# FFN 1's input projection with seven half-size products for eight (19 of 22 tiles), and another passage to the output projection in both FFNs

## The chip, the core and the metric

One NeuronCore of a Trainium2 chip runs the whole kernel. The metric is the device time of one execution in microseconds. The core has a matrix engine (PE, with its own weight loads PEld), a vector engine (DVE), a scalar engine (ACT), GpSimd (POOL) and SyncE (SP); the last two start most of the DMA transfers here. The engines work through lists of instructions of their own and wait for each other by semaphores.

## The reference

One layer of a decoder trunk over 1056 tokens (1024 of a prompt, 32 of eight sample sequences of 4), in fp32, with D = 1024 and a feed-forward width of 2816. `mod` is a normalisation followed by scale and shift; these and the gates come from a small product of a conditioning vector with a large weight matrix (called ada below, nine sets of 1024 numbers).

```
x += 1/2 * gate1 * swiglu(mod(norm(x), shift, scale), ffn1_w_in, ffn1_w_out)
x += gate2 * W_out(sig(gA) * DiffAttn(h) + sig(gB) * Retention(h))
x += 1/2 * gate3 * swiglu(mod(norm(x), shift, scale), ffn2_w_in, ffn2_w_out)
y  = norm(x)

def swiglu(h, w_in, w_out):          # w_in 1024 x 5632, w_out 2816 x 1024
    a, b = split(h @ w_in, 2, axis=-1)
    return (silu(a) * b) @ w_out
```

## The kernel before

**Products.** An fp32 matrix is kept as a high and a low part (`hh`/`hl` for activations, `..h`/`..l` for weights; `split`: the high part on ACT at L175, the low part on DVE at L185), and each product of two tiles is three matmuls (`mm3`, L234 to L236: high by high, high weight by low activation, low weight by high activation). Activations lie with features on the 128 partitions and the 1056 token columns behind them. The columns are taken in three blocks of 352 (`rb`; the last holds 320 prompt and 32 sample columns), in halves of 528 (HR) or in quarters of 264 (QR).

**Two ways of the input projection.** The 2816 hidden features are 22 tiles of 128. The plain way does a tile with two units (`pa`, `pb`) for each of three blocks, 24 matmuls of 352 columns each: 144 for a tile. `ffn_seven` treats the tile's a- and b-parts, the two halves of the 1024 input features and the two halves of the columns as a 2 by 2 block product and does it with seven products instead of eight: each is 24 matmuls of 264 columns, 168 for a tile. It needs sums and differences of the activation blocks (`sums`, `last_sum`, kept in `gx`, 50.7 KB a partition), of the weight blocks (`weights`, on DVE) and of the results (`p1`, `u2`, `p5` on DVE and ACT).

**FFN 1** (64 to 905 us) is one function, `ffn`: for each of six groups of tiles (`CHUNKS`) the plain input projection, with silu(a) times b split into `gh`/`gl` in on-chip memory, and then that group's part of the output projection (`po`), added to X at once by `residual` (L465 to L472). X stays on the chip. Into both kinds of work `step(more)` places the ada steps that are still open: each loads 512 KB of ada weights, splits them and gives PE four matmuls (`adap`); its three buffers are single.

**FFN 2** (2395 to 3149 us) has two tiles the plain way (`ffn_plain`), 20 by `ffn_seven`, with silu(a) times b written to DRAM (`gd`), and then the output projection of all 22 tiles (`ffn_out`), which reads `gd` back in groups (`gr`, `stage`). X lies in DRAM (`xd`) meanwhile and is read back as Z by eight transfers that POOL issues (L1614) before `ffn_out`.

**What sets the order.** The program is written as loops and generators; a list scheduler of the framework then fixes one order of instructions for each engine, and each engine keeps to it. SP's and POOL's transfers each stand in such an order too, so one that waits for its buffer holds up those behind it. Between the FFNs (905 to 2393 us) lie attention, retention and the mixer, which the change doesn't touch.

## Time and profile before

| | before |
|---|---|
| median of 3 runs | 3152.3 us (3148.41 to 3164.13) |
| the profiled execution | 3151.32 us, span in the trace 3149.6 us |
| matmuls on PE | 19615 |
| PE busy | 3013.9 us, 96% of the span |
| DVE / ACT / POOL busy | 57% / 39% / 16% |

The profile is of one execution. The span is the time from the first to the last instruction in it, so 1.7 us of the execution's own time lie outside. Busy times are those of an engine; an engine that is idle costs nothing unless the end waits for it. A few matmul records are missing from the trace.

### The profile page before, as it was taken

The page shows a single profiled execution, that of the slowest core. Times are in us where ns is not written, and L with a number is a line of the kernel's source. Part 1 is how long each engine was busy: PE and PEld are TensorE (multiplying, and loading weights), DVE is VectorE, ACT ScalarE, POOL GpSimd, SP SyncE. Part 2 cuts the span into 40 slices and gives each one's busy share as a digit, 9 for nine tenths or more (in the row PEclk, how much of TensorE's full clock was granted, in tenths as well). Part 3 has the DMA queues.
Part 4 walks back from the last instruction along what each step waited for, and adds up shares of the span by engine and source line. Part 5 has one row for each costly group of instructions (what it writes and reads, how often), then busy time and mean ns, then how long its engine had stood idle before and what let it go on. Part 6 is the DMA issues. An engine that isn't in the chain of part 4 may idle for free.

```text
span 3149.6 us, 49441 instructions
## 1 busy us (share of the span) xinstructions
PE 3013.9 (96%) x19615; PEld 2872.9 (91%) x19615; DVE 1801.1 (57%) x3555; ACT 1240.6 (39%) x2376; POOL 517.8 (16%) x680
## 2 busy tenths in 40 slices
PE   7999999999999999998999999998899999999998
PEld 3999999999989999998889998887798999999998
DVE  5443434344265666667767766666558755554555
ACT  5422222322244243335556556454445433332112
POOL 2100000000033223213223332232023000000002
PEclk9999999999999999999999999999999999999998
DMA  6232222221122313214121221225651222225321
GB/s 219 61 114 82 87 81 84 88 91 54 59 97 69 103 61 104 82 52 135 56 68 59 74 81 57 74 70 159 202 166 44 78 82 75 78 79 192 103 68 56
DMA packets 270130, 286.73 MB, mean 91 GB/s; under 512 B 14224, under 2 KB 224705, under 8 KB 269898
## 3 DMA queue, kind: packets, MB, share of 16 engines
q1 hardware_dynamic: 248394, 212.28, 22.2%
q0 software_dynamic: 21504, 71.29, 6.4%
q8 instruction: 154, 2.52, 0.3%
q14 instruction: 78, 0.64, 0.1%
HBM read 223.78 MB, written 59.74 MB: 90 GB/s over the span
## 4 chain that ended last, share of the span: by engine, by line
PE 36%; DVE 5%; issue 4%; ACT 4%; DMA 3%; POOL 2%; DVEq 0%; ACTq 0%; POOLq 0%; SPq 0%
PE po L235 3%; PE po L236 3%; PE po L234 3%; PE x L235 2%; PE x L234 2%; PE x L236 2%; PE gp L234 1%; PE gp L236 1%; PE gp L235 1%; PE q L235 1%; PE q L234 1%; PE q L236 1%; DMA k_prompt<-ko 1%; PE s L1319 1%; PE s L1320 1%
## 5 line engine op out<-in xcount | busy, mean ns | idle before, releaser
L494 DVE TENSOR_TENSOR silu<-silu,pb 128x352 f32<-128x352 f32 x66 | 34.4, 521 | 232.1 <-PE pb L236 230.0
L428 POOL TENSOR_TENSOR acc<-acc,sq 128x352 f32<-128x352 f32 x27 | 32.5, 1202 | 799.0 <-ACT sq L427 789.4
L465 DVE SCALAR_TENSOR_TENSOR X<-po,mod,X 128x352 f32<-128x352 f32 (+1 forms) x144 | 81.8, 570 | 111.3 <-PE po L236 110.8
L465 DVE SCALAR_TENSOR_TENSOR Z<-po,mod,Z 128x352 f32<-128x352 f32 (+1 forms) x144 | 81.7, 570 | 96.0 <-PE po L236 95.8
L1325 ACT ACTIVATE P<-s,mx 128x256 f32<-128x256 f32 (+7 forms) x128 | 94.7, 740 | 94.7 <-DVE mx L1323 86.3
L1323 DVE TENSOR_REDUCE mx<-s 128x1 f32<-128x256 f32 (+7 forms) x128 | 96.3, 754 | 2.5
L185 DVE TENSOR_TENSOR c<-s,c 128x512 fp32r<-128x512 f32 x80 | 55.2, 690 | 74.0 <-ACT c L175 73.6
L234 PE MATMUL x<-hh,c 128*128 128x264 f32 x320 | 91.8, 287 | 2.4 <-ACT hh L175 1.7
L175 ACT ACTIVATE gh<-silu 128x352 fp32r<-128x352 f32 x66 | 32.7, 496 | 154.8 <-DVE silu L494 154.6
L236 PE MATMUL x<-hh,c 128*128 128x264 f32 x320 | 91.3, 286 | 1.4 <-DVE c L185 1.4
L235 PE MATMUL x<-hl,c 128*128 128x264 f32 x320 | 91.8, 287 | 0.2 <-DVE hl L185 0.2
L235 PE MATMUL x<-gl,c 128*128 128x264 f32 x320 | 91.2, 285 | 0.0
L234 PE MATMUL x<-gh,c 128*128 128x264 f32 x320 | 91.1, 285 | 0.0
L236 PE MATMUL x<-gh,c 128*128 128x264 f32 x320 | 90.9, 285 | 0.0
L1319 PE MATMUL s<-kk,st 128*128 128x512 f32 (+2 forms) x192 | 69.8, 364 | 16.9 <-ACT P L1325 16.8
L175 ACT ACTIVATE ah<-at 128x512 fp32r<-128x512 f32 (+1 forms) x80 | 44.2, 553 | 57.9 <-PE at L1349 57.4
L493 ACT ACTIVATE silu<-pa 128x352 f32<-128x352 f32 x66 | 30.2, 457 | 92.8 <-PE pa L236 92.8
L234 PE MATMUL gp<-hh,g_1h 128*128 128x352 f32 x192 | 66.0, 344 | 0.0
L234 PE MATMUL gp<-hh,g_0h 128*128 128x352 f32 x192 | 65.4, 340 | 0.0
L1320 PE MATMUL s<-kl,st 128*128 128x512 f32 (+2 forms) x192 | 64.7, 349 | 0.4 <-ACT kl L1285 0.3
L236 PE MATMUL gp<-hh,g_1l 128*128 128x352 f32 x192 | 64.0, 333 | 0.0
L235 PE MATMUL gp<-hl,g_1h 128*128 128x352 f32 x192 | 63.7, 332 | 0.0
(1778 smaller groups left out, 11842.7 us busy)
## 6 DMA issues: line engine op xcount, KB each, us to landing
gr<-gd SPq DMA_DIRECT2D x22, 528.0 KB
ada_0r<-ada_w SPq DMA_DIRECT2D x18, 512.0 KB
ada_1r<-ada_w SPq DMA_DIRECT2D x18, 512.0 KB
ada_2r<-ada_w SPq DMA_DIRECT2D x18, 512.0 KB
ada_3r<-ada_w SPq DMA_DIRECT2D x18, 512.0 KB
st<-state_ret SPq DMA_DIRECT2D x32, 256.0 KB
state_ret_sample<-st POOLq DMA_DIRECT2D x32, 256.0 KB, 2.3
kp<-cache_k SPq DMA_DIRECT2D x64, 128.0 KB
```

The lines of the kernel that those rows point to most:

```text
L175: S.activation(out, in_, AF.Copy, scale=scale)
L185: (eng or V).tensor_tensor(out=l, in0=src, in1=f(h), op=ALU.subtract)
L234: T.matmul(out, wh, xh, start=first and j == 0, stop=False, **kw)
L235: T.matmul(out, wh, xl, start=False, stop=False, **kw)
L236: behind[0] = T.matmul(out, wl_, xh, start=False, stop=last and j == n - 1, **kw).ins
L428: (V if k % 2 else G).tensor_tensor(out=acc[k % 2], in0=acc[k % 2], in1=sq[:], op=ALU.add)
L465: V.scalar_tensor_tensor(out=x[k][:, c0:c0 + n], in0=p_[:, :n], scalar=gt[:, k, 0:1], in1=x[k][:, c0:c0 + n], op0=ALU.mult, op1=ALU.add)
L494: V.tensor_tensor(out=s_[:], in0=s_[:], in1=pb[:, :RB], op=ALU.mult)
L1319: T.matmul(ss[:, a:e], s_[:, qc], k_[:, a:e], start=True, stop=False)
L1320: T.matmul(ss[:, a:e], s_[:, qc], l_[:, a:e], start=False, stop=True)
L1323: V.tensor_reduce(out=mx[:], in_=ss[:, :wd], op=ALU.max, axis=AX.X, negate=True)
L1325: S.activation(pt[:, :wd], ss[:, :wd], AF.Exp, bias=mx[:], accum_out=rs[:, c:c + 1])
```

## The change

FFN 1 gets the structure of FFN 2. Its first three tiles are done the plain way (`ffn_plain`, the first two interleaved), tiles 3 to 21 by `ffn_seven` with two ada steps in each tile (`per` = 2, behind products 0 and 1), and `ffn_out` follows. X goes to DRAM as soon as it stands (`keep1`, three transfers on POOL's queue), gives its memory to `gx`, and is read back by eight transfers on SP's queue.

In both FFNs `ffn_out` has a new first group, of two tiles. Its activations are staged in halves of 528 columns in `hh`/`hl` 4 to 7, which the last tile of `ffn_seven` has read by the end of its second product, through the weights' raw buffers (`wr`); its output projection runs in four quarters of 264 columns (192 matmuls) where three blocks of 352 would take 144. X is read back from SP's queue behind the first output weights (in FFN 2 from POOL's queue before). The accumulation bank of the ada steps has a pool of its own and outlives the others (`stay`).

```diff
-CHUNKS = [[0, 1, 2, 3], [4, 5, 6, 7], [8, 9, 10, 11], [12, 13, 14, 15], [16, 17], [18, 19, 20, 21]]
-CHUNKS2 = [[0, 1, 2, 3], [4, 5, 6, 7], [8, 9, 10, 11], [12, 13, 14, 15], [16, 17, 18, 19], [20, 21]]
+CHUNKS = [[0, 1], [2, 3, 4, 5], [6, 7, 8, 9], [10, 11, 12, 13], [14, 15, 16, 17], [18, 19, 20, 21]]
+CHUNKS2 = [[0, 1], [2, 3, 4, 5], [6, 7, 8, 9], [10, 11, 12, 13], [14, 15, 16, 17], [18, 19], [20, 21]]
...
     def residual(tp, x, k, rb, p_, gt):
+        residual_at(tp, x, k, rb * RB, RB, p_, gt)
+
+    def residual_at(tp, x, k, c0, wd, p_, gt):
+        n = min(wd, SEQ - c0)
...
-    def ffn_out(w, tp, x, wout, gt, after, chunks, homes, bridge=iter(()), more=iter(())):
+    def ffn_out(w, tp, x, wout, gt, after, chunks, reload, bridge=iter(()), more=iter(())):
+        def parts(t, ci, q):
+            return t[(4 if ci % 2 == 0 else 0) + q]
         def stage(ci):
             for q, ft in enumerate(chunks[ci]):
-                r = tp.tile([P, ROWS], F32, tag="gr", name=f"gr{ft}", bufs=2)
-                ld(out=r[:], in_=gd[ft][:, :])
-                split(*(t[:] for t in homes[ci][q]), r[:])
+                if ci == 0:
+                    for c in range(2):
+                        r = w.p.tile([P, 8, P], F32, tag="wr", name=f"gr{ft}{c}", bufs=w.raw)[:].rearrange("p k c -> p (k c)")[:, :HR]
+                        ld(out=r, in_=gd[ft][:, c * HR:(c + 1) * HR])
+                        split(*half(4 + 2 * q + c, 0), r)
+                else:
+                    r = tp.tile([P, ROWS], F32, tag="gr", name=f"gr{ft}", bufs=2)
+                    ld(out=r[:], in_=gd[ft][:, :])
+                    split(parts(hh, ci, q)[:], parts(hl, ci, q)[:], r[:])
                 yield
...
+                if ci == 0:
+                    c, s = divmod(rb, 2)
+                    mm3(p_[:, :QR], ws, [tuple(t[4 + 2 * q + c][:, s * QR:(s + 1) * QR] for t in (hh, hl)) for q in range(nf)])
+                    residual_at(tp, x, o, rb * QR, QR, p_, gt())
...
                 for ct in range(nf):
                     step(more)
                     wt = w.get(rows[:, ct * cw:(ct + 1) * cw], nf, cw, f"wo{ci}_{ct}")
+                    if ci == 0 and ct == 0:
+                        reload()
...
+        def keep1(X, rb, eng):
+            eng(out=xd[:, rbs(rb)].rearrange("(k p) c -> p k c", p=P), in_=X[:, :, rbs(rb)])
+        def entry():
+            yield from norm(tn, X, 2, mods, 1, 0, tp)
+            for rb in range(NRB):
+                keep1(X, rb, st)
+            xs1.close()
+            gx.extend(quarters(tas, side="right"))
+            gx.append(pool(tas, "ta", side="right"))
...
-        ffn(sc, w, tp, x, i["ffn1_w_in"][0], i["ffn1_w_out"][0], lambda: mods[2], after1, CHUNKS, LEAD, to_ret(), more,
-            pre={(0, 0): norm(tp, X, 1, mods, 1, 0), (PQ, 1): norm(tp, X, 2, mods, 1, 0)})
+        ffn_plain(w, tp, win1, [0, 1, 2], LEAD, {(0, 0): norm(tn, X, 1, mods, 1, 0, tp), (PQ, 1): entry()}, todo, more, LEAD)
+        for _ in todo:
+            pass
+        psum(0, 0, 1, True)
+        ffn_seven(w, gx[3], gx, win1, list(range(3, DFF // P)), last_sum(gx[3], gx), more, 2)
+        tas.close()
+        psum(3, 3, 1, True)
+        X1 = pool(sb_, "xb", side="right").tile([P, KT, ROWS], F32, name="X1")
+        x = [X1[:, k, :] for k in range(KT)]
+        def reload():
+            for k in range(KT):
+                ld(out=x[k], in_=xd[k * P:(k + 1) * P, :])
...
+        ffn_out(w, pool(sb_, "t1b", side="right"), x, i["ffn1_w_out"][0], lambda: mods[2], after1, CHUNKS, reload, to_ret(), more)
...
-            for k in range(KT):
-                st(out=x[k], in_=xd[k * P:(k + 1) * P, :])
-            ffn_out(w3, pool(s2, "t3"), x, i["ffn2_w_out"][0], lambda: mods[8], after2, CHUNKS2,
-                    [[(hh[c % 2 * 4 + q], hl[c % 2 * 4 + q]) for q in range(4)] for c in range(len(CHUNKS2))])
+            def reload2():
+                for k in range(KT):
+                    ld(out=x[k], in_=xd[k * P:(k + 1) * P, :])
+            ffn_out(w3, pool(s2, "t3"), x, i["ffn2_w_out"][0], lambda: mods[8], after2, CHUNKS2, reload2)
```

The scheduler's order shows three places. The first is POOL at the start of the program, where the sums of squares of x (`acc`) of the three column blocks are added up; before:

```order
L428 TENSOR_TENSOR acc_0_349<-acc_0_349,sq_2_353 128x352
L786 DMA xn_335<-x_sample 32x1024
L428 TENSOR_TENSOR acc_0_349<-acc_0_349,sq_4_359 128x352
L428 TENSOR_TENSOR acc_0_349<-acc_0_349,sq_6_365 128x352
L428 TENSOR_TENSOR acc_1_640<-acc_1_640,sq_2_644 128x352
```

and now:

```order
L436 TENSOR_TENSOR acc_0_358<-acc_0_358,sq_2_362 128x352
L751 DMA xn_344<-x_sample 32x1024
L436 TENSOR_TENSOR acc_0_358<-acc_0_358,sq_4_368 128x352
L769 DMA xd<-X 128x8x352
L436 TENSOR_TENSOR acc_0_358<-acc_0_358,sq_6_374 128x352
L769 DMA xd<-X 128x8x352
L436 TENSOR_TENSOR acc_1_637<-acc_1_637,sq_2_641 128x352
L769 DMA xd<-X 128x8x352
L436 TENSOR_TENSOR acc_1_637<-acc_1_637,sq_4_647 128x352
```

The three stores of X moved ahead of the sums of blocks 1 and 2: they are issued as soon as X stands and not where `entry` is written.

The second place is PE in tile 12 of FFN 1, where an ada step ends one set of numbers and the next step begins; `x`, `q` and `y` are the accumulators of the seven products, `c2` and `c6` weight blocks. Now:

```order
L244 MATMUL y12_1_3774<-hh7_138,c212_3670 128x264
L390 MATMUL adap3_1_3344<-pick_214,ab_212 128x36
L242 MATMUL x12_0_3769<-gh10_914,c612_3705 128x264
L243 MATMUL x12_0_3769<-gl10_915,c612_3705 128x264
L244 MATMUL x12_0_3769<-gh10_914,c612_3705 128x264
L242 MATMUL x12_0_3769<-gh11_916,c612_3705 128x264
L243 MATMUL x12_0_3769<-gl11_917,c612_3705 128x264
L244 MATMUL x12_0_3769<-gh11_916,c612_3705 128x264
L414 MATMUL adap5_0_3858<-ada5_0_0h_3818,cs_148 18x512
L414 MATMUL adap5_0_3858<-ada5_0_0l_3819,cs_148 18x512
L414 MATMUL adap5_0_3858<-ada5_0_0h_3818,cs_148 18x512
```

The ada matmuls, which before stood among the matmuls of `pa`, `pb` and `po` of FFN 1, now stand behind products 0 and 1 of each seven-product tile, 24 matmuls of 264 columns apart (in this tile the second stands six matmuls into product 2).

The third place is DVE in the first group of FFN 2's output projection, where the results `po` are added to X (there called Z); before:

```order
L185 TENSOR_TENSOR wo1_0l_29321<-wo1_0r_29318,wo1_0h_29320 128x1024
L465 SCALAR_TENSOR_TENSOR Z_28890<-po0_4_0_29124,mod8_5472,Z_28890 128x352
L465 SCALAR_TENSOR_TENSOR Z_28890<-po0_4_1_29138,mod8_5472,Z_28890 128x352
L465 SCALAR_TENSOR_TENSOR Z_28890<-po0_4_2_29152,mod8_5472,Z_28890 128x320
L470 TENSOR_TENSOR rs4_29166<-po0_4_2_29152,mod8_5472 128x32
L472 TENSOR_TENSOR Z_28890<-Z_28890,rs4_29166 128x32
```

and now:

```order
L193 TENSOR_TENSOR wo1_1l_30711<-wo1_1r_30708,wo1_1h_30710 128x1024
L475 SCALAR_TENSOR_TENSOR Z_30272<-po0_4_3_30484,mod8_7027,Z_30272 128x232
L480 TENSOR_TENSOR rs4_30492<-po0_4_3_30484,mod8_7027 128x32
L475 SCALAR_TENSOR_TENSOR Z_30272<-po0_5_0_30495,mod8_7027,Z_30272 128x264
L482 TENSOR_TENSOR Z_30272<-Z_30272,rs4_30492 128x32
L475 SCALAR_TENSOR_TENSOR Z_30272<-po0_5_1_30503,mod8_7027,Z_30272 128x264
L475 SCALAR_TENSOR_TENSOR Z_30272<-po0_5_2_30511,mod8_7027,Z_30272 128x264
L193 TENSOR_TENSOR hl2_141<-gr4_30530,hh2_133 128x1056
```

An output tile takes four accumulating instructions and two short ones on DVE where it took three and two, for half as many hidden tiles, and the low parts of the next group's activations (`hl2<-gr4`) lie between them. In the whole of the new first group DVE has, beside 32 of the accumulating and 16 of the short instructions, five low parts of 1056 columns and two of 1024-column weights in FFN 2; in FFN 1 five, and three (two of them ada's).

## Rows read from the trace of the kernel before

**Rows 1.** The page: busy time, TensorE's granted clock, the last chain.

```profile
PE 3013.9 (96%) x19615; PEld 2872.9 (91%) x19615; DVE 1801.1 (57%) x3555; ACT 1240.6 (39%) x2376; POOL 517.8 (16%) x680
...
PEclk9999999999999999999999999999999999999998
...
PE 36%; DVE 5%; issue 4%; ACT 4%; DMA 3%; POOL 2%; DVEq 0%; ACTq 0%; POOLq 0%; SPq 0%
```

**Rows 2.** Windows of FFN 1 and seven: all engines, PEclk, DMA share, GB/s.

```profile
60.00:905.00 845.00, 832.74 (x5065) 795.19 (x5064) 362.84 (x598) 247.69 (x411) 30.49 (x28) 1.00 0.25 77
2474.00:2857.00 383.00, 383.00 (x3138) 383.00 (x3137) 202.58 (x387) 147.16 (x318) 22.55 (x43) 1.00 0.27 85
```

**Rows 3.** Timeline, DVE: last gate of FFN 1's plain tiles 20 and 21.

```profile
821.75 0.52 DVE L494 TENSOR_TENSOR silu<-silu,pb 128x352 f32<-128x352 f32 x1 [1.72 <-PE pb L236]
...
844.64 0.52 DVE L494 TENSOR_TENSOR silu<-silu,pb 128x352 f32<-128x352 f32 x1 [1.72 <-PE pb L236]
```

**Rows 4.** Timeline, POOL: stores of FFN 2's seven-product tiles, twelve tiles apart.

```profile
2610.88 0.54 POOL L672 DMA_DIRECT2D gd<-p  x1 [17.71 <-DVE p L667]
...
2855.56 0.55 POOL L672 DMA_DIRECT2D gd<-p  x1 [4.91 <-DVE p L667]
```

**Rows 5.** Timeline, PE: first and last of six ada waits (idle in brackets).

```profile
138.65 0.41 PE L406 MATMUL adap<-ada_3h,cs 128*18 128x512 f32 x1 [0.77 <-ACT ada_3h L175]
...
191.28 0.40 PE L406 MATMUL adap<-ada_3h,cs 128*18 128x512 f32 x1 [0.42 <-ACT ada_3h L175]
```

**Rows 6.** Timeline, PE and ACT: FFN 2's passage to the output projection.

```profile
2858.12 0.42 PE L234 MATMUL po<-hh,wo_0h 128*128 128x352 f32 x1 [0.84 <-ACT hh L175]
...
2866.68 0.85 PE L234 MATMUL po<-hh,wo_0h 128*128 128x352 f32 x3 [2.59 <-ACT hh L175]
...
2865.54 1.08 ACT L175 ACTIVATE hh<-gr 128x1056 fp32r<-128x1056 f32 x1 [6.03 <-DMA gr<-gd]
```

**Rows 7.** Windows: that passage (PE alone), four us of it (all engines).

```profile
2858.10:2882.00 23.90, 19.98 (x91) 0.79 0.84 316
...
2870.00:2874.00 4.00, 4.00 (x15) 4.00 (x15) 2.19 (x6) 0.00 (x0) 0.00 (x0) 0.50 1.03 407
```

**Rows 8.** Startup: windows, the later store of X (DMA), one ada load and split.

```profile
20.00:40.00 20.00, 17.57 (x73) 7.58 (x74) 11.90 (x17) 13.63 (x27) 6.24 (x7) 0.91 1.03 344
40.00:60.00 20.00, 14.56 (x36) 5.14 (x35) 15.82 (x20) 13.14 (x24) 8.18 (x5) 0.78 0.86 262
60.00:80.00 20.00, 18.31 (x97) 14.05 (x96) 16.60 (x23) 14.45 (x31) 5.03 (x5) 0.96 0.08 30
...
xd<-Y POOLq DMA_DIRECT2D x3, 1408.0 KB, 6.9
...
44.47 0.37 SPq L203 DMA_DIRECT2D ada_3r<-ada_w  x1
...
54.35 1.04 ACT L175 ACTIVATE ada_3h<-ada_3r 128x1024 fp32r<-128x1024 f32 x1
```

**Rows 9.** Window: FFN 2's entry into the seven products, all engines.

```profile
2439.30:2474.00 34.70, 30.21 (x225) 28.64 (x224) 32.05 (x57) 14.58 (x30) 1.57 (x3) 0.96 0.26 74
```

**Rows 10.** Groups of FFN 1: the parts of an ada step.

```profile
L185 DVE TENSOR_TENSOR ada_3l<-ada_3r,ada_3h 128x1024 fp32r<-128x1024 f32 x14 | 17.1, 1225 | 8.6 <-ACT ada_3h L175 8.6
...
L175 ACT ACTIVATE ada_3h<-ada_3r 128x1024 fp32r<-128x1024 f32 x13 | 13.6, 1050 | 22.8 <-DMA ada_3r<-ada_w 22.8
```

**Rows 11.** Groups of FFN 2's output projection on DVE.

```profile
L465 DVE SCALAR_TENSOR_TENSOR Z<-po,mod,Z 128x352 f32<-128x352 f32 x76 | 43.9, 581 | 53.2 <-PE po L236 53.2
L465 DVE SCALAR_TENSOR_TENSOR Z<-po,mod,Z 128x320 f32<-128x320 f32 x37 | 20.3, 550 | 35.4 <-PE po L236 35.4
L185 DVE TENSOR_TENSOR hl<-gr,hh 128x1056 fp32r<-128x1056 f32 x16 | 20.1, 1256 | 12.1 <-ACT hh L175 12.1
L472 DVE TENSOR_TENSOR Z<-Z,rs 128x32 f32<-128x32 f32 x38 | 7.2, 190 | 1.1
L470 DVE TENSOR_TENSOR rs<-po,mod 128x32 f32<-128x32 f32 x38 | 6.8, 180 | 0.0
```

More of the change, by code (lines that the diff above doesn't have):

```diff
@@ L126, in build, with psum @@
     banks = [None]
-    def psum(mm, aux, big):
+    bigs = [None]
+    def psum(mm, aux, big, stay=False):
         if banks[0]:
             banks[0][0].close()
+        if not stay:
+            if bigs[0]:
+                bigs[0][0].close()
+            es = ExitStack()
+            bigs[0] = (es, pool(es, "psb", space=PSUM), big)
         es = ExitStack()
-        banks[0] = (es, pool(es, "ps", space=PSUM), mm, aux, big)
+        banks[0] = (es, pool(es, "ps", space=PSUM), mm, aux)
     psum(3, 3, 1)
@@ L143, in big_ps @@
     def big_ps(name):
-        return banks[0][1].tile([P, 1024], F32, tag="big", name=name, bufs=banks[0][4])
+        return bigs[0][1].tile([P, 1024], F32, tag="big", name=name, bufs=bigs[0][2])
     xd = dr.tile([KT * P, ROWS], F32, name="xd")
@@ L470, in residual @@
             V.tensor_tensor(out=t[:].rearrange("p (b t) -> p b t", t=TS),
[L471 removed]
+                            in0=p_[:, n:wd].rearrange("p (b t) -> p b t", t=TS), in1=bc(gt, k), op=ALU.mult)
             V.tensor_tensor(out=xs, in0=xs, in1=t[:], op=ALU.add)
[L474 to L530 removed]
@@ L532, in ffn_plain @@
-    def ffn_plain(w, tp, win, fts, lead, pre, back=iter(()), more=iter(())):
+    def ffn_plain(w, tp, win, fts, lead, pre, back=iter(()), more=iter(()), quiet=0):
         ws = {}
@@ L542, in ffn_plain @@
             pb = unit(ws[q][1], rb, f"pb{ft}_{rb}")
-            for _ in range(2 - rb % 2):
+            for _ in range((q, rb) == (quiet - 1, 2) if q < quiet else 2 - rb % 2):
                 step(more)
@@ L692, in ffn_out @@
             rows = wout[f0 * P:(f0 + nf) * P, :]
-            g = homes[ci]
             nxt = stage(ci + 1) if ci + 1 < len(chunks) else iter(())
@@ L698, in one @@
                 cc = (o * P) % cw
-                mm3(p_[:, :RB], [(wt[0][:, q, cc:cc + P], wt[1][:, q, cc:cc + P]) for q in range(nf)],
-                    [(g[q][0][:, rbs(rb)], g[q][1][:, rbs(rb)]) for q in range(nf)])
-                residual(tp, x, o, rb, p_, gt())
+                ws = [(wt[0][:, q, cc:cc + P], wt[1][:, q, cc:cc + P]) for q in range(nf)]
+                if ci == 0:
+                    c, s = divmod(rb, 2)
+                    mm3(p_[:, :QR], ws, [tuple(t[4 + 2 * q + c][:, s * QR:(s + 1) * QR] for t in (hh, hl)) for q in range(nf)])
+                    residual_at(tp, x, o, rb * QR, QR, p_, gt())
+                else:
+                    mm3(p_[:, :RB], ws, [tuple(parts(t, ci, q)[:, rbs(rb)] for t in (hh, hl)) for q in range(nf)])
+                    residual(tp, x, o, rb, p_, gt())
             if ci < len(chunks) - 1:
@@ L706, in ffn_out @@
                     wt = w.get(rows[:, ct * cw:(ct + 1) * cw], nf, cw, f"wo{ci}_{ct}")
+                    if ci == 0 and ct == 0:
+                        reload()
                     for o in range(ct * cw // P, (ct + 1) * cw // P):
-                        for rb in range(NRB):
+                        for rb in range(4 if ci == 0 else NRB):
                             one(wt, o, rb)
-                    next(nxt, None)
+                        if o % 2:
+                            next(nxt, None)
                 run(nxt)
@@ L769, in build @@
     bridge = []
-    with ExitStack() as sc:
+    with ExitStack() as sc, ExitStack() as sb_:
         xp = pool(sc, "x1", side="right")
@@ L775, in build @@
         V.tensor_tensor(out=pick[:], in0=quarter(0), in1=quarter(9), op=ALU.add)
-        X = xp.tile([P, KT, ROWS], F32, name="X")
+        xs1, tas, gx = ExitStack(), ExitStack(), []
+        X = pool(xs1, "xa", side="right").tile([P, KT, ROWS], F32, name="X")
+        tn = pool(xs1, "n1", side="right")
         tp = pool(sc, "t1")
-        x = [X[:, k, :] for k in range(KT)]
         with ExitStack() as s2:
@@ L801, in build, with back @@
                         (7, "scale", gff2, False), (6, "shift", None, False), (8, "half", None, False)])
-        def after1(tp, rb):
-            yield from norm(tp, X, rb, mods, 4, 3)
-            (st if rb == 2 else ld)(out=xd[:, rbs(rb)].rearrange("(k p) c -> p k c", p=P), in_=X[:, :, rbs(rb)])
+        def keep1(X, rb, eng):
[7 more added lines that the diff above has]
+            gx.append(pool(tas, "ta", side="right"))
+        def back():
+            while not gx:
+                yield
+            yield from sums(gx[3], gx)
         def rv_pair(r):
```

84 lines of the change are left out of this document (15 added, 69 removed).

## The prediction, on record before the run

> **What bounds the kernel now.** I read the page first: PE is busy 96% of the span, the next engine, DVE, 57%, and PE's granted clock is at its upper level in all slices but the last [rows 1]. The chain that ended last gives PE only 36%, far less than that; it shows one path and is no account of where the span goes. So the question for each stage is how many matmuls it has, what one costs, and where PE stands still. The windows answer the last: FFN 1's 845 us hold 832.7 us of PE work with DVE busy 43%, the seven-product stretch of FFN 2 holds 383.0 of 383.0 with DVE at 53% [rows 2]. Both stages are PE's, so fewer PE cycles there are time, as long as no other engine takes over.
>
> What a tile costs in each way is read from events one tile apart, not from counts of records, since some are missing. The last gate of a plain tile without an ada step is at 821.75, the next one's at 844.64: 22.9 us for 144 matmuls, 159 ns for one of 352 columns [rows 3]. Twelve seven-product tiles lie between the stores at 2610.88 and 2855.56: 244.68 / 12 = 20.4 us for 168 matmuls, 121.4 ns for one of 264 columns [rows 4].
>
> **Tiles 3 to 21 of FFN 1 by seven products.** 22.9 - 20.4 = 2.5 us for a tile, times 19: **-47.5**. The gain in columns is an eighth, in time 11%: the two prices lie on a line of 0.427 ns a column and 8.7 ns a matmul, and that fixed part is paid 168 times for 144. The Trainium skill, page "TensorE: Matmul & The Clock Gate", section "Back-to-back issue gap", speaks against the change: it gives a stream of weight loads and matmuls some 81 ns at 128 columns and 131 ns at 512. Estimated on a line between them that page would give 110 ns at 352 and 99 ns at 264, so 15.9 us for a plain tile and 16.6 for a seven-product one, +13 us in all. The trace does not agree with that page: it has 159 and 121 ns.
>
> **The ada steps.** Their matmuls are the same ones in another place. What goes is six waits in the first group of FFN 1's output projection, where PE stood for a split; the first is 0.77, the last 0.42, all six 3.1 us [rows 5]: **-3.1**. What comes is two steps a tile through single buffers. Step B stands one product (24 x 0.1214 = 2.9 us) behind step A, and its splits can't start before A's matmuls are done: 1.05 on ACT and 1.22 on DVE, 2.3 us [rows 10], so 0.6 us is left for the queue on DVE. From below nothing; from above each of 19 tiles waits as those six did on average, 19 x 0.51 = 9.7. I take **+2**, near the lower end, since 2.3 is under 2.9. If a wait comes, the seven's next product on PE is late, and nothing else.
>
> **The passage to the output projection in FFN 2.** Before, PE waits 0.84 us for the first split part of `hh`, and 2.59 for a later one, whose transfer came 6.03 us after ACT was free for it [rows 6]. The 23.9 us from 2858.1 hold 91 matmuls, at 159 ns 14.5 us of work, and late in them the granted clock is 0.50, the lower of the two levels (1.2 GHz), after an engine that stood still [rows 7]. So 9.4 us and the first wait are lost, 10 us. The cause in the trace is transfers: Z and `gr` together kept the share of the DMA engines at 1.03 [rows 7]. Now two half-size tiles are staged while PE is in the last seven-product tile, and Z is behind the first weights on SP. **-10**, if PE goes from the one to the other without a stop. Z's and `gr`'s bytes are then under way in products 5 and 6 and the new first group (6 + 23 us); before they took some 20 us at about 400 GB/s [rows 7]; I cost them at nothing. If that cover is too short, `po` results wait for X, PE's three accumulators fill up, and up to the same 10 us come back.
>
> **The new first group** is PE work of 192 x 0.1214 = 23.3 us for 144 x 0.159 = 22.9: +0.4 for each FFN, **+0.8**. But DVE gets more to do. From 581 ns at 352 columns and 550 at 320 the slope is 0.97 ns a column, so (an estimate) 496 ns at 264 and 465 at 232. An output tile is 3 x 0.496 + 0.465 + 0.18 + 0.19 = 2.3 us, eight 18.6; five low parts of 1.256 are 6.3 [rows 11], two weights or ada low parts of 1.22 [rows 10] 2.4, and small ones some 0.8: 28.2 against 23.3 of PE in FFN 2; in FFN 1 one low part more, 29.4, against 23.3 and two ada steps (eight matmuls of 512 columns, on the line above 1.8 us), 25.1. So DVE is the longer by 4 to 5 us. Three accumulators let it lag by 3 x 0.73 = 2.2 us, and chunk 1, with twice the matmuls for a result, lets it catch up. I take **+3 for each**. From below nothing (the first results may meet an idle DVE); from above 10 each, the loss of the old passage.
>
> **X stored at startup.** In FFN 1 X now goes out and comes back. The scheduler puts the three stores of 1408 KB among POOL's first sums, in the first 60 us of the kernel. There the DMA engines are full: their share is 1.03 from 20 to 40 us at 344 GB/s, 0.86 to 60, 0.08 after that, while an ada load issued at 44.47 is split only at 54.35 [rows 8]. PE is at 73% from 40 to 60, waiting for these loads. 4.3 MB at 344 GB/s are 12.6 us of transfer. If all of it came before loads that PE waits for, the start would end 12.6 us later; if it fell behind them into the empty time after 60, nothing. The Trainium skill, page "Trainium Kernel Development and Optimization", section "Key Constraints", says that transfers started from SP and from POOL run on the same 16 engines and interleave. By that page the stores are taken from the loads' rate. I take **+2.5**: a part of the loads is done before X stands, so the stores can only be in the way of the rest. What is late next is ada's first two sets of numbers, and with them FFN 1's first matmul.
>
> **Entry into the seven products.** The sums of activations need DVE while the plain tiles run. In FFN 2 the entry's 34.7 us hold 225 matmuls, at 121.4 ns 27.3 us, with DVE busy 32.05 of 34.7 [rows 9]: up to 7.4 us lost. FFN 1 has three plain tiles for the sums, but also ada's low parts. Between 0 and 7.4 I take **+3**.
>
> **Sum**, against the profiled execution (3151.3, 1 us under the median of the three): -47.5 - 3.1 - 10 + 0.8 + 2 + 3 + 3 + 2.5 + 3 = -46.3, so **3105 us**. The middle stage, FFN 2's seven products and both tails keep their instructions.
>
> **The rivals.**
> - *Unknown costs near their upper ends.* The stores (12.6 for 2.5) and DVE in the first groups (10 for 3, twice) would add 24 us: some 3129. For it speaks the full DMA share; against it that PE's stall in the old passage came from DMA, and DVE was not its cause. With one of the two, 3115 to 3119.
> - *All of it is hidden:* 3105 - 13.5 = 3091.5.
> - *The passage of FFN 2 gives nothing:* 3115. For it: X's read waits for memory of the sums as before, on the queue that also brings `gr`.
> - *The other side: ada's splits stop PE in every seven-product tile.* PE would wait for both splits at both steps, 2 x 2.3 = 4.5 us, times 19 = 87 less the 2 counted: 3190. It decides at 2.4 us a tile: there the change gives nothing against 3151; from 3.3 it is slower by over 0.5%. For it: single buffers, and an ACT and a DVE that carry the seven's own work. Against it: with the same buffers FFN 1 of before had six waits in all, 0.51 us each [rows 5], if at steps that stood further apart.
> - *The price of a matmul is a fixed one for the most part.* Tiles would then cost more by seven products; without gain the fixed part would be 0.427 x 264 = 113 ns, where the trace's line has 8.7. With the two prices that the other rule gives, +13 us for -47.5, the time would be about 3166. That is the rule of the page "TensorE: Matmul & The Clock Gate" of the Trainium skill; the trace does not agree, so it gets 0.01.
>
> **How the numbers follow.** The forecast and its neighbourhood, 3097 to 3113: 0.60. One of the big unknowns near its upper end, or the passage without gain, 3113 to 3122: 0.17. Several, up to 3136: 0.08. All hidden, below 3097: 0.09. Ada's stop in every tile 0.05, half of it within 0.5% and half slower; the fixed price 0.01, within 0.5%. A measurement of this kernel tells about 0.5%, 16 us, from no change, so faster means below 3136.5. Faster: 0.60 + 0.17 + 0.08 + 0.09 = 0.94; same 0.035; slower 0.025. The range from 3094 to 3124 leaves out some 0.04 below and 0.12 above.
>
> **What would show it.** In the profile after: stores of tiles 4 to 21 in FFN 1 20.4 us and two ada steps (22.2) apart, PE busy throughout, and no `adap` matmul with idle time before it (step ada); `po` of FFN 2 beginning without a wait and PE's clock at its upper level there (passage); idle time of PE before the first groups' matmuls, released by DVE (first group); the first `pa` matmul later than before by what the stores cost. I would be wrong if the seven-product tiles of FFN 1 lay over 24 us apart, if FFN 1's matmuls began more than 6 us later, or if PE stood still over 10 us in either first group.

## The result, and the profile after

The changed kernel takes **3110.94 us** (median of 4 runs, 3107.88 to 3111.67) against 3153.83 us for the kernel before in the same runs: a ratio of 0.9858, 95% interval [0.9832, 0.9885], 43 us less. 3105 was predicted, with a range of 3094 to 3124. The profiled execution has a span of 3109.7 us, 39.9 less than before.

The page after, with PE's busy time and its granted clock, answers to [rows 1]:

```profile
PE 2968.7 (95%) x20167; PEld 2830.2 (91%) x20167; DVE 1974.0 (63%) x3935; ACT 1325.9 (43%) x2580; POOL 540.5 (17%) x722
...
PEclk8999999999999999999999999999999999999999
```

There are 552 matmuls more, and PE is busy for 45 us less; DVE took 173 us more. Where the 39.9 us come from is read by cutting both spans at the same five places: FFN 1's first matmul, an early matmul of retention (`rv`) where FFN 1 ends, the mixer's last product, the first seven-product matmuls of FFN 2 and the end of its last one. The windows of before (length; PE's busy time and matmuls; granted clock; DMA share; GB/s):

```profile
0.00:64.32 64.32, 43.61 (x155) 0.89 0.81 267
64.32:905.40 841.08, 829.59 (x5055) 1.00 0.25 77
905.40:2368.34 1462.94, 1388.01 (x8990) 0.99 0.30 94
2368.34:2439.42 71.08, 64.21 (x369) 0.95 0.13 45
2439.42:2857.96 418.54, 413.37 (x3361) 1.00 0.27 84
2857.96:3149.60 291.64, 275.09 (x1692) 0.95 0.29 98
```

and the same of after:

```profile
0.00:73.36 73.36, 44.79 (x154) 0.86 0.83 293
73.36:867.85 794.49, 784.44 (x5562) 0.99 0.38 119
867.85:2335.67 1467.82, 1390.01 (x8989) 0.99 0.30 93
2335.67:2406.76 71.09, 63.97 (x370) 0.95 0.13 45
2406.76:2826.05 419.29, 414.76 (x3361) 0.99 0.27 84
2826.05:3109.70 283.65, 270.77 (x1742) 0.98 0.31 101
```

| stretch | measured | predicted |
|---|---|---|
| start, up to FFN 1's first matmul | +9.0 | +2.5 |
| FFN 1 | -46.6 | -42.2 (-47.5 - 3.1 + 0.4 + 2 + 3 + 3) |
| attention, retention, mixer | +4.9 | 0 |
| FFN 2: plain tiles and seven products | +0.8 | 0 |
| FFN 2: passage, output projection, end | -8.0 | -6.6 (-10 + 0.4 + 3) |
| sum | -39.9 | -46.3 |

The gain is where the sum put it, in FFN 1's tiles and FFN 2's passage. Two stretches took back more than was counted, the start and a middle whose instructions did not change. Of the last row's 8.0 us, 5.6 lie before the last `po` (270.48 us and 264.92 us from the end of the last product); the other 2.4 lie in the tail behind it, where both kernels have the same instructions.

### The profile page after: what moved, and what is told of

It is laid out like the page before. It is cut to its first block, busy times and chain, and to the rows that moved or that the text cites. A ratio compares the mean times of both kernels' runs of the same rounds, so it can differ in the third digit from the quotient of the medians.

```text
span 3109.7 us, 51457 instructions
## 1 busy us (share of the span) xinstructions
PE 2968.7 (95%) x20167; PEld 2830.2 (91%) x20167; DVE 1974.0 (63%) x3935; ACT 1325.9 (43%) x2580; POOL 540.5 (17%) x722
## 4 chain that ended last, share of the span: by engine, by line
PE 36%; issue 5%; DVE 4%; ACT 4%; DMA 3%; POOL 2%; DVEq 0%; POOLq 0%; ACTq 0%; SPq 0%
PE x L244 2%; PE x L242 2%; PE x L243 2%; PE po L242 2%; PE po L243 2%; PE po L244 2%; PE gp L242 1%; PE gp L243 1%; PE gp L244 1%; PE q L242 1%; PE q L243 1%; PE q L244 1%; DMA k_prompt<-ko 1%; PE s L1316 1%; PE s L1317 1%
## 5 line engine op out<-in xcount | busy, mean ns | idle before, releaser
L242 PE MATMUL x<-hh,c 128*128 128x264 f32 x624 | 179.0, 287 | 2.6 <-ACT hh L183 1.7
L244 PE MATMUL x<-hh,c 128*128 128x264 f32 x624 | 178.3, 286 | 1.5 <-DVE c L193 1.5
L242 PE MATMUL x<-gh,c 128*128 128x264 f32 x624 | 178.2, 286 | 0.0
L244 PE MATMUL x<-gh,c 128*128 128x264 f32 x624 | 177.3, 284 | 0.0
L242 PEld LDWEIGHTS x<-hh,c 128*128 128x128 f32 x624 | 118.8, 191 | 3.8 <-ACT hh L183 1.9
L244 PEld LDWEIGHTS x<-hh,c 128*128 128x128 f32 x624 | 118.9, 191 | 1.8 <-DVE c L193 1.7
L242 PEld LDWEIGHTS x<-gh,c 128*128 128x128 f32 x624 | 117.4, 188 | 2.4
L243 PEld LDWEIGHTS x<-hl,c 128*128 128x128 f32 x624 | 118.8, 190 | 0.5 <-DVE hl L193 0.4
L243 PEld LDWEIGHTS x<-gl,c 128*128 128x128 f32 x624 | 117.3, 188 | 0.9
L244 PEld LDWEIGHTS x<-gh,c 128*128 128x128 f32 x624 | 117.4, 188 | 0.2
L183 ACT ACTIVATE c<-s 128x512 fp32r<-128x512 f32 x156 | 97.6, 626 | 41.6 <-PE y L244 24.5
L242 PE MATMUL po<-hh,wo_0h 128*128 128x352 f32 (+1 forms) x328 | 105.0, 320 | 4.8 <-DVE X L475 4.6
L242 PE MATMUL po<-hh,wo_1h 128*128 128x352 f32 (+1 forms) x328 | 104.8, 319 | 2.9 <-DVE rs L480 1.7
L183 ACT ACTIVATE hh<-gr 128x1056 fp32r<-128x1056 f32 (+1 forms) x48 | 47.5, 1009 | 133.1 <-DMA gr<-gd 68.8
L243 PE MATMUL po<-hl,wo_0h 128*128 128x352 f32 (+1 forms) x328 | 104.1, 317 | 0.0
```

The costliest lines, as they stand in the source:

```text
L183: S.activation(out, in_, AF.Copy, scale=scale)
L242: T.matmul(out, wh, xh, start=first and j == 0, stop=False, **kw)
L243: T.matmul(out, wh, xl, start=False, stop=False, **kw)
L244: behind[0] = T.matmul(out, wl_, xh, start=False, stop=last and j == n - 1, **kw).ins
```

## The experiments

**The start.** In the windows of the start the DMA engines now stay full to 60 us and are at 0.40 for 20 us more, where [rows 8] had 0.08 (all engines, then clock, DMA share, GB/s):

```profile
20.00:40.00 20.00, 15.97 (x68) 7.19 (x69) 10.32 (x16) 12.64 (x24) 8.05 (x10) 0.87 1.07 388
40.00:60.00 20.00, 11.13 (x23) 2.96 (x22) 11.05 (x14) 8.60 (x18) 2.83 (x4) 0.76 0.94 339
60.00:80.00 20.00, 15.49 (x60) 8.42 (x59) 13.88 (x18) 14.34 (x28) 4.99 (x5) 0.86 0.40 129
```

The timeline of POOL, SP, ACT and PE shows how it reached PE:

```profile
28.37 0.96 POOL L769 DMA_DIRECT2D xd<-X  x1
...
42.28 5.23 SPq L211 DMA_DIRECT2D ada_0r<-ada_w  x1
...
50.76 1.06 ACT L183 ACTIVATE ada_0h<-ada_0r 128x1024 fp32r<-128x1024 f32 x1 [5.08 <-DMA ada_0r<-ada_w]
...
54.39 1.03 ACT L420 COPY ab<-adap 9x128 f32<-9x128 f32 x4
...
55.48 0.64 PE L390 MATMUL adap<-ident,ab 128*128 128x36 f32 x2 [6.16 <-ACT ab L420]
```

With the later stores under way (each takes some 10.7 us from issue to landing), an ada load takes 5.23 us to be issued, ACT waits 5.08 us for it, the copies that end ada's first set stand behind that split in ACT's order, and PE stands still for 6.16 us. POOL's own time for the issues is not what PE waits for here: behind the third store POOL itself stands idle for 11.70 us, until ACT gives it the next square. Two theories fit, the stores' bytes (A) and the order that the scheduler makes with the stores in it (B), and a third is that neither did it (C). *late_stores* queues the stores on POOL behind the last low part that POOL makes in the first norm (`lows` lists these instructions):

```diff
+            with tc.issue_after(lows[3]):
                 for rb in range(NRB):
                     keep1(X, rb, st)
```

> The changed kernel with the three stores of X queued on POOL behind the low parts of block 0's norm, so that they start at about 73 us, where the DMA engines have little to do, and not at 28 us. Theory A (the stores' 4.3 MB take the rate from the loads that PE waits for at the start) and theory B (the stores make the scheduler order ACT, DVE and PE otherwise at the start) both expect FFN 1's first matmul back at 64 to 67 us from 73.4, and 6 to 9 us less than the changed kernel, some 3103 us. Theory C (something else of the change moved the start, such as the pools on the other side of the memory) expects it to stay at 73. If the sums of FFN 1 then wait for the stores to leave X's memory, the gain is given back before tile 3: the first seven-product matmul would not come earlier than 154.

*before_plus_stores* and *before_plus_half_stores* do nothing but add the stores to the kernel before:

```diff
+        def keep():
+            yield from norm(tp, X, 2, mods, 1, 0)
+            for rb in range(NRB):
+                st(out=xd[:, rbs(rb)].rearrange("(k p) c -> p k c", p=P), in_=X[:, :, rbs(rb)])
...
-            pre={(0, 0): norm(tp, X, 1, mods, 1, 0), (PQ, 1): norm(tp, X, 2, mods, 1, 0)})
+            pre={(0, 0): norm(tp, X, 1, mods, 1, 0), (PQ, 1): keep()})
```

and, for half stores, in the place of the st:

```diff
-                st(out=xd[:, rbs(rb)].rearrange("(k p) c -> p k c", p=P), in_=X[:, :, rbs(rb)])
+                for a in (0, 4):
+                    st(out=xd[a * P:a * P + 512, rbs(rb)].rearrange("(k p) c -> p k c", p=P), in_=X[:, a:a + 4, rbs(rb)])
```

> The kernel before with nothing but the three stores of X added at the start (as the change places them; nobody reads them). Theories A and B: first matmul of FFN 1 at about 73 us for 64.3, the time 9 us longer, some 3162. Theory C: 64 us and no change of time.

> The kernel before with the same 4.3 MB stored as six stores of half the size, with which the scheduler keeps nearly the order of before on PE, DVE, ACT and SP (4, 4, 8 and 2 rows of the first 120 differ, where 18, 24, 34 and 6 do with three large ones). Theory A (bytes): the first matmul of FFN 1 at 71 to 75 us all the same. Theory B (order): 64 to 67 us.

FFN 1's first matmul in the timelines of the three, in that order:

```profile
64.68 0.49 PE L242 MATMUL pa<-hh,wa0h 128*128 128x352 f32 x1
```

```profile
74.23 0.49 PE L234 MATMUL pa<-hh,wa0h 128*128 128x352 f32 x1
```

```profile
70.94 0.32 PE L234 MATMUL pa<-hh,wa0h 128*128 128x352 f32 x1
```

Theory C falls: stores alone move the first matmul of the kernel before by 9.9 us (one execution, 3171.24 us, 17 more where 9 were expected; some 6 of the rest lie in FFN 1, and their cause was not looked for), and without them at the start the changed kernel begins at 64.7. Between A and B the half stores decide for the larger part: nearly the old order and the same bytes cost 6.6 us (one execution, 3165.18 us). The order with three large stores goes with the other 3.3.

*late_stores* took 3106.10 us (ratio to before 0.9842, interval [0.9825, 0.9858]), 5 under the changed kernel by the medians and not 9 (the four times of each overlap). Its first seven-product matmul came at 148.66, 84.0 us behind the first matmul, against 81.0 in the changed kernel. Theory D blamed POOL, which issues the stores between the low parts of the norms, theory E a DVE that is full in any case. *stores_on_sp* has SP issue them behind the last ada load:

```diff
             run(ada(w0, [(1, "scale", gff1, True), (0, "shift", None, False)]))
+            start_loads = W.last
...
-            for rb in range(NRB):
-                keep1(X, rb, st)
+            with tc.issue_after(start_loads):
+                for rb in range(NRB):
+                    keep1(X, rb, ld)
```

> The changed kernel with the three stores of X issued by SP behind the last ada load of the start, so that they run from about 57 us and POOL is free for the low parts of the norm. Late stores on POOL brought the first matmul from 73.4 to 64.7 us, but tile 3 came only 5.7 us earlier: 3 us were given back in the plain tiles. Theory D: POOL's issues of the stores (0.9 us each) and POOL's late low parts gave it back; then here tile 3 begins at 146 and the time is 8 us under the changed kernel's. Theory E: DVE is what the entry into the seven products waits for (sums, norms, ada's low parts), whoever issues the stores; then tile 3 begins at 148 to 149 again, and the time is some 5 us under the changed kernel's.

Its timeline, SP and PE:

```profile
55.05 5.55 SPq L770 DMA_DIRECT2D xd<-X  x3
...
62.28 0.33 PE L242 MATMUL pa<-hh,wa0h 128*128 128x352 f32 x1
...
142.59 0.28 PE L242 MATMUL x<-hh,c 128*128 128x264 f32 x1
```

80.3 us lie between the two matmuls, so nothing was given back, as theory D has it and theory E does not. That POOL's issues were the cause is not shown: in this stretch PE waits for POOL's low parts for 1.3 us in *late_stores* and 1.2 here. What went are waits for an ada split of ACT's (2.7 us for 1.0) and for its part `hh` (1.4 for 0.2), and the stores also run earlier. The span is 8.8 us under the changed kernel's, the median 3104.64 us (ratio 0.9842 [0.9826, 0.9858]), 6 under.

*sp_stores_quiet* also moves four of the third plain tile's five ada steps to later places:

```diff
-        ffn_plain(w, tp, win1, [0, 1, 2], LEAD, {(0, 0): norm(tn, X, 1, mods, 1, 0, tp), (PQ, 1): entry()}, todo, more, LEAD)
+        ffn_plain(w, tp, win1, [0, 1, 2], LEAD, {(0, 0): norm(tn, X, 1, mods, 1, 0, tp), (PQ, 1): entry()}, todo, more, 3)
```

> As stores_on_sp, and the third plain tile of FFN 1 takes one ada step for five; the other four come later, in the seven-product tiles' sequence and the output projection. Theory E (DVE sets the entry): four low parts of 1.2 us less on DVE and no ada split on ACT behind the sums' splits, so tile 3 begins about 4 us of ada matmuls and 2 to 4 us of waits earlier, and the whole gains 2 to 4 us against stores_on_sp. Theory D: only the ada matmuls move, and the time is the same within 1 us.

3098.67 us (ratio 0.9824 [0.9808, 0.9841]). The first seven-product matmul came at 136.76, 75.6 us behind the first matmul, but FFN 1 as a whole became only 0.3 us shorter (from the first matmul to retention's first, 808.1 for 808.5). In FFN 1 the matmuls moved and that was all, as theory D has it. The median is 6 us lower all the same, and the four times of each kernel don't overlap; between the two profiled executions, 5.2 us apart, the middle stage (below) is 4.8 us shorter, and whether this edit does that stays open. Whether DVE is near its limit in the entry was asked again with *two_plain_tiles*, on top of *six_accumulators* (below):

```diff
-        ffn_plain(w, tp, win1, [0, 1, 2], LEAD, {(0, 0): norm(tn, X, 1, mods, 1, 0, tp), (PQ, 1): entry()}, todo, more, 3)
+        ffn_plain(w, tp, win1, [0, 1], LEAD, {(0, 0): norm(tn, X, 1, mods, 1, 0, tp), (PQ, 1): entry()}, todo, more, 2)
...
-        ffn_seven(w, gx[3], gx, win1, list(range(3, DFF // P)), last_sum(gx[3], gx), more, 2)
+        ffn_seven(w, gx[3], gx, win1, list(range(2, DFF // P)), last_sum(gx[3], gx), more, 2)
```

> As six_accumulators, with two plain tiles in FFN 1 and 20 by seven products. By matmuls alone 2.5 us less. Theory E (DVE sets the entry): in sp_stores_quiet DVE is busy 70.7 of the 75.6 us of the three plain tiles; without the third it still has some 66 us to do, so the first seven-product matmul can't come before some 130 us where the two tiles end at 113, and the time is some 15 us longer than with three.

3115.11 us in one execution, 16 over the profiled one of *six_accumulators*. The seven products began early, at 116.3 and not behind 130, and then waited in their first tiles: from FFN 1's first matmul to its first `po` it took 519.2 us where three plain tiles took 508.9. So it became 10.3 us longer where the matmuls alone give 2.5 less, and the windows of the entry and of 12 us in it show why. DVE is busy for 64.26 of 69.00 us and PE for 61.38; from 118 to 130 us DVE is busy throughout, PE stands still for 4.8 us, and its granted clock is 0.59 on the mean, for the most part the lower of its two levels (PE, PEld, DVE, ACT, POOL, clock):

```profile
61.00:130.00 69.00, 61.38 (x342) 55.66 (x343) 64.26 (x106) 38.24 (x71) 17.69 (x18) 0.90 0.23 82
...
118.00:130.00 12.00, 7.20 (x30) 6.58 (x31) 12.00 (x21) 3.15 (x6) 0.54 (x1) 0.59 0.05 17
```

**Ada's steps.** In the timeline after, tiles 5 and 20 of FFN 1 are stored 15 tiles apart, 336.39 / 15 = 22.43 us for a tile with two ada steps:

```profile
223.42 0.54 POOL L625 DMA_DIRECT2D gd<-p  x1 [17.71 <-DVE p L620]
...
559.81 0.54 POOL L625 DMA_DIRECT2D gd<-p  x1 [17.58 <-DVE p L620]
```

That is 2.03 us over FFN 2's tile without one (20.4), 1.0 for a step, and not the 4.5 more of the rival. In the kernel before a plain tile with two steps took 25.03 us (last gates at 400.88 and 425.91), 2.1 over one without. *ada_steps_together* takes the cover away:

```diff
-                if j < per:
-                    step(more)
+                for _ in range(per if j == 0 else 0):
+                    step(more)
```

> The changed kernel with both ada steps of each seven-product tile behind product 0 (behind products 0 and 1 before). The scheduler then sets the second step's first matmul nine product matmuls (1.1 us) behind the first step's last. If one product of 2.9 us is the cover that hid the second step's splits (2.3 us), PE waits some 1.2 us or more in each of 19 tiles, 23 us or more in all, and the tiles' stores stand some 23.6 us apart for 22.4. Rival: the splits have slack elsewhere and the distance does not matter; then under 3 us in all.

The stores of three tiles that follow each other:

```profile
224.15 0.54 POOL L625 DMA_DIRECT2D gd<-p  x1 [17.78 <-DVE p L620]
247.18 0.54 POOL L625 DMA_DIRECT2D gd<-p  x1 [18.27 <-DVE p L620]
269.63 0.54 POOL L625 DMA_DIRECT2D gd<-p  x1 [17.66 <-DVE p L620]
```

23.03 and 22.45 us by turns, where the changed kernel has 22.51 and 22.33: 0.3 a tile on the mean, FFN 1 5.8 us longer, where 23 were expected (3115.90 us, one execution). The expectation took both splits onto the path, and PE does not wait for them. The short gap of 1.1 us lies in the tiles of 22.45 us, which lost 0.12. The tiles of 23.03 us lost 0.52; in these a set of numbers ends between the two steps, and PE waits for ACT's copies of its results:

```profile
231.67 0.41 PE L390 MATMUL adap<-pick,ab 128*128 128x36 f32 x2 [0.25 <-ACT ab L420]
```

From 220 to 560 us these are the only waits of PE that the profile lists, eight of them and 2.0 us in all, where the changed kernel has none. So no wait for a split shows, as the rival has it; the 5.8 us are over its 3, and they come for the most part from the tiles in which a set ends.

**FFN 2's passage alone.** *ffn2_passage_alone* is the kernel before with the new `ffn_out`, `residual_at`, `CHUNKS2` and Z's read on SP, used by FFN 2 only:

```diff
-CHUNKS2 = [[0, 1, 2, 3], [4, 5, 6, 7], [8, 9, 10, 11], [12, 13, 14, 15], [16, 17, 18, 19], [20, 21]]
+CHUNKS2 = [[0, 1], [2, 3, 4, 5], [6, 7, 8, 9], [10, 11, 12, 13], [14, 15, 16, 17], [18, 19], [20, 21]]
...
-            for k in range(KT):
-                st(out=x[k], in_=xd[k * P:(k + 1) * P, :])
+            def reload2():
+                for k in range(KT):
+                    ld(out=x[k], in_=xd[k * P:(k + 1) * P, :])
```

> The kernel before with the new passage to the output projection in FFN 2 alone. If the terms add up, 7 us less than before (10 of stalls gone, 0.4 more matmul time, some 2.5 of waits for DVE in the new first group), about 3146 against 3153, and PE goes from the last product to the first output matmul without a wait. Rival: the passage gains nothing by itself, because Z's read and the other loads have the same bytes to move in the same time; then within 2 us of before, and PE waits for the first results' place.

3148.72 us against 3154.29, ratio 0.9981 [0.9971, 0.9990]: 5.6 us less (its time alone is used here, so that PE goes on without a wait was seen in the changed kernel only). That agrees with the 6.6 of the prediction and with the 5.6 us that the changed kernel gained before its last `po`.

**The new first group.** In the changed kernel PE goes on to the first `po` without a wait where [rows 6] had 0.84, and its granted clock stays at the upper level where [rows 7] had 0.50. What waits there are, the larger ones, stand in the timeline of PE, of FFN 1 and FFN 2, and the low parts before the last two in that of DVE:

```profile
603.97 0.36 PE L242 MATMUL po<-hh,wo_1h 128*128 128x264 f32 x1 [0.75 <-DVE rs L480]
...
2840.79 0.36 PE L242 MATMUL po<-hh,wo_1h 128*128 128x264 f32 x1 [0.99 <-DVE rs L480]
2842.37 0.39 PE L242 MATMUL po<-hh,wo_1h 128*128 128x264 f32 x1 [0.61 <-DVE Z L475]
...
2838.92 1.26 DVE L193 TENSOR_TENSOR hl<-gr,hh 128x1056 fp32r<-128x1056 f32 x1 [0.78 <-ACT hh L183]
...
2840.56 1.25 DVE L193 TENSOR_TENSOR hl<-gr,hh 128x1056 fp32r<-128x1056 f32 x1
```

They are DVE's, in the bunches of low parts. DVE's price of a quarter was estimated well, 490 ns in its group for 496:

```profile
L475 DVE SCALAR_TENSOR_TENSOR Z<-po,mod,Z 128x264 f32<-128x264 f32 x21 | 9.9, 490 | 1.9 <-PE po L244 1.9
```

*sp_quiet_pool_lows* takes the low parts of the second group from DVE, on top of *sp_stores_quiet*:

```diff
-                    split(parts(hh, ci, q)[:], parts(hl, ci, q)[:], r[:])
+                    four = [t[:].rearrange("p (k c) -> p k c", k=4) for t in (parts(hh, ci, q), parts(hl, ci, q), r)]
+                    split(*four, eng=G if ci == 1 else None)
```

> As sp_stores_quiet, and the low parts of the second group's activations (four of 1056 columns in each FFN) are made on POOL for DVE. If the waits in the new first groups (2.3 us in FFN 2, 2.9 in FFN 1) are those of DVE for bunches of low parts, they go, and the time is 3 to 5 us under sp_stores_quiet. Rival: the groups wait for gr's and X's transfers, then no change; or POOL is so much slower that the second group waits for it, then PE stands still at the second group's first matmul.

It was not faster: 3105.04 us (0.9846 [0.9829, 0.9862]), 6 over *sp_stores_quiet*. PE's waits for DVE went from 2.3 to 1.5 us in FFN 2's first group, but in FFN 1's, up to the beginning of the second group, from 1.5 to 3.3. That is a part of the 6 us only. The timeline of DVE and POOL shows a reason that neither theory had:

```profile
2833.48 1.31 DVE L482 TENSOR_TENSOR Z<-Z,rs 128x32 f32<-128x32 f32 x1
...
2836.10 1.23 DVE L482 TENSOR_TENSOR Z<-Z,rs 128x32 f32<-128x32 f32 x1
...
2828.59 6.15 POOL L191 TENSOR_TENSOR hl<-gr,hh 128x528 fp32r<-128x528 f32 x4 [10.09 <-PE po L244]
...
2835.95 2.60 POOL L191 TENSOR_TENSOR hl<-gr,hh 128x528 fp32r<-128x528 f32 x2 [1.21 <-ACT hh L183]
```

The 32-column add that takes 0.19 us [rows 11] takes 1.31 and 1.23 while POOL makes its low parts; the first of the two ends at 2834.79, when POOL's four subtractions end (2834.74). The Trainium skill, page "SBUF — State Buffer", section "Who interferes with whom", says that a DVE instruction with two inputs from that memory contends with a GpSimd instruction that reads it, and that the pair of ports they share is locked by one of them. The trace agrees with that, 1.1 us at a time: the add has two such inputs (Z and `rs`), and the accumulating instructions, which read one such tile beside `po`, keep their mean of 488 ns.

*six_accumulators* leaves the low parts on DVE and gives PE more room:

```diff
-                p_ = aux_ps(f"po{ci}_{o}_{rb}")
+                p_ = (mm_ps if ci == 0 and rb % 2 else aux_ps)(f"po{ci}_{o}_{rb}")
```

> As sp_stores_quiet, with six accumulators instead of three for the results of the new first group (the three of the input projection, free there, take every other quarter). If PE's waits in the first groups (1.6 us in FFN 1, 2.8 in FFN 2 in one stretch each) are those for a result that DVE has not yet taken, three more results of 0.73 us cover bunches of 2.5 us of low parts: the waits go, DVE lags and catches up in the second group, and the time is 3 to 5 us under sp_stores_quiet. Rival: DVE is short of time altogether (28 to 29 us of work against 23 to 25 of PE), then the waits only come later and the gain is under 1 us.

The window of FFN 2's first group and what follows has no idle time of PE left, where *sp_stores_quiet* at the same place (first row) has 37.44 us busy of 40:

```profile
2811.00:2851.00 40.00, 37.44 (x274) 36.28 (x273) 31.94 (x68) 11.35 (x11) 0.54 (x1) 1.00 0.82 278
...
2817.00:2857.00 40.00, 40.00 (x298) 39.91 (x298) 34.20 (x73) 11.66 (x11) 0.54 (x1) 1.00 0.83 282
```

From the first `po` of FFN 2 to the first output transpose it takes 242.4 us for 246.2. FFN 1's output projection gained 0.8. So the waits were for the place of a result, DVE has time enough over two groups, and the rival falls. With 3094.95 us (median of three, 3093.77 to 3098.67), ratio 0.9804 [0.9784, 0.9823], this is the best version, 16 us under the changed kernel and 3.7 under *sp_stores_quiet*, whose times it overlaps with; its profiled execution has the middle 5.8 us longer.

**The middle.** From attention's first `gp` to the mixer's first `wop` the kernel before took 685.5 us and the changed one 692.2, with the same order of instructions. The change moves the accumulators to other banks; *accumulators_moved* does that alone to the kernel before:

```diff
+        bigs[0] = pool(es, "psb", space=PSUM)
         banks[0] = (es, pool(es, "ps", space=PSUM), mm, aux, big)
...
-        return banks[0][1].tile([P, 1024], F32, tag="big", name=name, bufs=banks[0][4])
+        return bigs[0].tile([P, 1024], F32, tag="big", name=name, bufs=banks[0][4])
```

> The kernel before with the ada accumulator in a pool of its own, which moves all accumulators to other banks, as the change does, and nothing else. The unchanged stage from the end of the attention's first products to the mixer's last product took 685.5 us before and 692.2 after. Theory F (the place of the accumulators costs it): 690 to 693 here. Theory G (it is not the change but the run: the stage's transfers land a little earlier or later each time): 685 to 688 here, or any value between 685 and 694.

689.6 us (3161.76 us in all, one execution), just under theory F's values and among those that theory G allows, so it decides nothing. *changed_again* profiled the changed kernel once more:

> The changed kernel unaltered, profiled a second time, for the unchanged stage between attention's first products and the mixer's last (685.5 us in the kernel before, 692.2 in the changed one, 685.5 to 689.6 in the kernels made from the kernel before, 688.2 to 696.1 in those made from the changed one). Theory G (the stage varies from run to run): a value that differs from 692.2 by over 2 us. Theory H (the changed program itself is slower there, by a mechanism not found): 691 to 693. The first matmul of FFN 1 again at 73 to 74 us.

The stage's ends in its timeline:

```profile
1512.03 0.40 PE L242 MATMUL gp<-hh,g_1h 128*128 128x352 f32 x1
...
2200.89 0.66 PE L242 MATMUL wop<-hh,wo0h 128*128 128x352 f32 x1 [7.08 <-ACT wo0h L183]
```

688.9 us, 3.3 less than the first time: theory G for at least that much. (FFN 1's first matmul came at 74.60, 1.2 us later than the first time.) Over all profiles read the kernel before and the three made from it have 685.5, 686.7, 687.8 and 689.6, the changed one and those made from it 688.2 to 696.1. PE's windows of the stage show what differs (before, after, *accumulators_moved*, *six_accumulators*; length, busy time and matmuls, granted clock):

```profile
1549.03:2234.55 685.52, 635.09 (x4062) 0.98 0.29 89
...
1510.15:2202.37 692.22, 638.28 (x4062) 0.98 0.28 87
...
1553.26:2242.83 689.57, 638.98 (x4063) 0.97 0.29 88
...
1499.84:2194.70 694.86, 641.89 (x4063) 0.97 0.28 87
```

PE's busy time for the same matmuls goes from 634.7 to 642.2 us, in both groups higher where the mean granted clock is lower; that is the larger part of the spread. PE's idle time is 50.4 to 52.0 us in the four of the first group (50.6 in *accumulators_moved*, so the accumulators' place adds none) and 52.0 to 54.5 in the nine profiles of the second. So the changed program may be some 2 us slower here; why stays open.

## Why the prediction was right, and where its terms were off

**The main term held.** The tiles stand 22.43 us apart with two ada steps in each, where 22.2 was forecast from the rows of FFN 2. PE's busy time in FFN 1 fell by 45.2 us (829.59 to 784.44), 47.1 by the sum (47.5 less 0.4). So the rival of a price that is mostly fixed falls. With it falls, for these matmuls, the rule of the Trainium skill, page "TensorE: Matmul & The Clock Gate", section "Back-to-back issue gap", that stood behind it: by an estimate from its figures the tiles would have cost 13 us more.

**FFN 1's idle time was overestimated.** It went from 11.5 to 10.1 us, -1.4, where the sum had +4.9 (-3.1 of waits gone, +2 for ada, +3 for the entry, +3 for the first group). Ada's steps cost what they cost before, about 1 us each in either place, so its +2 was nothing. The entry was idle for 1.9 us (79.07 of 81.00 busy), of which 1.6 are waits for the norm's parts, where the kernel before has 2.4, and the seven-product tiles for 1.1 (428.58 of 429.70); so the entry's +3 was nearly nothing too, and that hangs on the third plain tile (*two_plain_tiles*). The first group lost 1.5 (26.40 of 27.94 busy) for 3. One limit of the rival on ada's splits was also worked out wrong: with the 2 us that the sum already holds, the change gives nothing at 2.5 us a tile and not at 2.4.

**The passage and the first group.** The two and the 0.4 of matmuls, -6.6 together, came out as -5.6 before the last `po` in the changed kernel; *ffn2_passage_alone* has -5.6 in all. The first group of FFN 2 was idle for 2.0 us (21.95 of 23.95 busy) for 3. The step that named DVE's bunches of low parts and three accumulators as the cause was right too (*six_accumulators*); that POOL could relieve DVE was not in the prediction, and *sp_quiet_pool_lows* did not gain by it. The tail, which the sum took as unchanged, gave 2.4 us more, and no run shows why.

**The stores at the start were mis-sized: +9.0 for +2.5.** The step took a value near the lower bound, because "the stores can only be in the way of the rest" of the loads. The rest became what PE waits for: the loads of ada's second set. The upper bound from the DMA rate (12.6) was the nearer one, and a start more than 6 us later is one of the signs that the prediction itself named for being wrong. The step also misread why PE was at 73% from 40 to 60 us [rows 8]: its waits there in the kernel before are 4.3 us for POOL's sums and 1.0 for ACT's copies, none for a load, and ACT waits 0.3 us for loads from 30 us to FFN 1's first matmul. The full DMA share of 1.03 was the sign that the loads had little slack; with the stores ACT waits 11.1 us for them in the same stretch, and PE 9.0 for ACT's copies behind that. The Trainium skill, page "Trainium Kernel Development and Optimization", section "Key Constraints", has transfers from POOL and SP run on the same engines and interleave; the runs agree with it, since stores on POOL's queue delay loads on SP's (the 5.08 us of ACT above).

**The middle was taken as 0.** It cost 4.9 in the profiled execution. In part that is variation of a stage of some 690 us: the same program took 3.3 us less in it the second time. Some 2 us may be the change's, and no run shows a cause for them.

The misses of the start and the middle (+6.5 and +4.9) and the gains in FFN 1 and at the end (-4.4 and -1.4) offset each other in part, so the sum came within 7 us. That closeness is partly luck; without the stores' error the time would have been nearer to 3105.

## What to carry to other kernels

Saving data to DRAM "on the side" is not free where the DMA engines are full: here it cost 9 us at a share of 1.03, though hardly anything had waited for those loads before. Read the share first, and where it is full, queue the stores behind the loads that come next on the path; SP's queue did better here than POOL's (80.3 for 84.0 us up to the seven products), for a reason that is not shown. When an engine lags in bunches, spare accumulators can be worth more than moving its work to another engine: six for three took PE's idle time in FFN 2's first group to nothing, while POOL's help slowed some of DVE's instructions. A price per matmul read from events one tile apart in one stage carried over to another: 45.2 us less work on PE where 47.1 were forecast.

## What the runs showed that was not expected

- POOL's subtractions of 528 columns stretch DVE's additions beside them: one of 32 columns from 0.19 to 1.31 us.
- An unchanged stage of some 690 us differs by 3.3 us between two executions of the same program (692.2 and 688.9), and by 10.6 between the kernels of this study, the larger part of it with the granted clock. A difference of a few microseconds in one profile is no proof of an edit.
- The order of instructions reacts to the size of a transfer: the same bytes in six stores for three kept nearly the whole order of the start, and the first matmul came 3.3 us earlier with it.
